# Attention tiles and upper banks in two pools each, and heads kind by kind

## The chip, the cores and the metric

One core of a Trainium2 chip runs the kernel. The metric is the device time of one execution in microseconds (us). The core has a matrix engine (TensorE, "PE" in the profile, with its weight loads as "PEld"), three engines for elementwise work (VectorE "DVE", ScalarE "ACT", GpSimd "POOL"), and a queue that issues transfers (SyncE, "SP"). Tiles live in SBUF; matmuls write PSUM, which has eight banks of 2 KB per partition.

## What is computed

Two layers of a streaming encoder over 1024 tokens of width 1024. Each layer runs three groups of four attention heads on one input projection, then attention over 256 memory tokens, then an MLP:

```python
for layer in range(DEPTH):
    h = rms_norm(x, mix_norm_g[layer])
    proj = h @ w_in[layer]
    da_q, da_k, da_v, sb_q, sb_k, sb_v, c_q, c_kv, k_r = jnp.split(proj, pts, axis=-1)
    y_a = diff_attention(da_q, da_k, da_v, rel_bias, da_q_norm_g[layer], da_k_norm_g[layer],
                         da_lambda[layer], da_subln_g[layer], layer)
    y_b = stick_breaking(sb_q, sb_k, sb_v, sb_out_g[layer])
    y_c = latent_attention(c_q, c_kv, k_r, pos, mla_cq_norm_g[layer], mla_ckv_norm_g[layer],
                           w_mla_uq[layer], w_mla_ukv[layer], mla_q_norm_g[layer],
                           mla_k_norm_g[layer], mla_out_g[layer])
    y = jnp.concatenate([y_a, y_b, y_c], axis=-1)
    x = x + y @ w_out[layer]
    h = rms_norm(x, memx_norm_g[layer])
    x = x + memory_attention(h, mem, mem_norm_g[layer], w_mem_q[layer], w_mem_kv[layer],
                             mem_q_norm_g[layer], mem_k_norm_g[layer], w_mem_o[layer])
    h = rms_norm(x, ffn_norm_g[layer])
    x = x + jnp.square(jax.nn.relu(h @ w_ff1[layer])) @ w_ff2[layer]
```

Differential attention takes softmax(map 0) - lam * softmax(map 1) and latent attention one softmax, each over the keys of earlier and the own chunk of 64. Stick-breaking attention uses a sigmoid and a running product instead of a softmax:

```python
log_beta = jax.nn.log_sigmoid(z)
log_1m_beta = jnp.where(earlier, jax.nn.log_sigmoid(-z), 0.0)
later = lax.cumsum(log_1m_beta, axis=3, reverse=True) - log_1m_beta
a = jnp.where(earlier, jnp.exp(log_beta + later), 0.0)
```

## The kernel before

**Two halves.** The 1024 tokens are eight tiles of 128 rows; half h = 0 is tiles 0 to 3, half 1 tiles 4 to 7. Half 0 attends to 512 keys at most, half 1 to 1024. A layer runs, in the order in which it is written: `project(0)`, the norm of half 1, the memory's keys and values (`memory`), `project(1)`, `attention(0)`, `merge(0)` (output projection and memory attention of half 0), `attention(1)`, `merge(1)`, and the MLP. The projections write queries, keys and values to DRAM (`dqk`, `sqk`, `mqk`, `dv`, `sv`, `mv`), and each head loads its own from there. Weights come as raw fp32 tiles of 128x512 (`raw`) and are split on ScalarE and VectorE into a high and a low part (lines 562 and 563), so that three matmuls make one product (`mm3`, lines 584 to 586).

**The order of each engine is made when the program is built.** `order_engines` (line 227) takes all instructions with their dependences and gives each engine a fixed list, by a list scheduling with estimated costs (`_cost`, line 192). Among the instructions that are ready it takes the one of lowest rank (`mem.rank`), and of equal rank the one that was written first. A layer's projection of half 0 has rank 0, merge(0) 9, attention(0) 10, project(1) 20, attention(1) 40, merge(1) 50 and the MLP 60. So project(1) fills the gaps of attention(0), and the first ten groups of the MLP on half 0 fill those of attention(1): `ff1` and `ff2` with the banks s2 and s3. The engines work through their lists in order.

**Places in SBUF.** Pools are stacked from two sides: left ones upward, right ones downward. A pool that is opened on the place of a closed one may be written only when the old one's uses are over; `order_engines` lets the first write of each tile wait for all uses of the closed pools under its pool (lines 112 and 281), and the chip's own waits go tile by tile. Above the fixed pools the kernel has 85.5 KB per partition. The inputs of the projections and of the MLP are one 32 KB tile for each half: `h0` at the left end, `h1` at the right end. The merge has a pool `mw` of 21 KB left, above h0.

- `attention(0)` has one pool, at0, of 39 KB on the left: over h0's place and 7 KB beyond.
- `attention(1)` has one pool, at1, of 52 KB on the right: over h1's place and over most of mw's.

In such a pool the tiles are: kst (keys of a head, 4 buffers in half 0, 6 in half 1), v (values, 2 or 3), o (queries, high and low part, and the bias of a differential head, 6 or 7), and in half 0 also p (3) and at (2) for the weights and their transposes; in half 1 these two come from the ring t4 of the fixed pools. A differential head takes 2 kst, 5 o and 1 v, a stick-breaking head 1, 2 and 1, a latent head 2, 2 and 1. Buffers are taken in turn.

**Banks.** Four banks (s0 to s3) are fixed. The upper four are one pool, `more` (lines 385 to 387): e0 to e3 during attention(0) and both projections, d0 and d1 of two banks each during attention(1) and the MLP. attention(0) and merge(0) use e0 and e1, the projection of half 1 and the memory e2 and e3.

**A head.** For each tile of its half: scores on TensorE (line 1019) into e0 or e1 (half 1: d0 or d1). Differential: a bias on the last 256 keys (1098, its tile loaded at 1086), the maximum (1099), Exp on ScalarE (1101), both maps joined (1107). Stick-breaking: two Sigmoids on ScalarE (1124, 1125), a scan on VectorE (1129), products on GpSimd (1128, 1131). Latent: maximum (1150), Exp (1153). Then transposes (605), a copy or a split by ScalarE and VectorE (1037, 597, 598), weighting (1039, 1054 to 1057) and a norm (1073 to 1076). The loads are at lines 980 (kst), 986 (latent kst and o), 992 (o) and 999 (v). Lines 1161 to 1163 run the twelve heads in turn by kind: head d of each kind, then head d + 1.

Of the kernel before, what the change touches and what calls it, by code (L numbers as in the profile page):

```python
# [9 lines left out]
F32 = mybir.dt.float32  # L10
F32R = mybir.dt.float32r
# [3 lines left out]
PSUM = bass.MemoryType.PSUM  # L15
DRAM = bass.MemoryType.DRAM

P = 128
# [331 lines left out]
def trunk(ctx: ExitStack, mem: Mem, tc: tile.TileContext, a: dict, out: bass.AP):  # L350
    nc = tc.nc
    HT = NT // 2
    HS = S // 2
# [8 lines left out]
    def f(ap):  # L362
        return ap.bitcast(F32)
# [13 lines left out]
    psp = Pool("psum", space=PSUM)  # L377
# [2 lines left out]
    turn = {}  # L380
    ALL, FRONT, BACK = ("s0", "s1"), ("s0", "s1", "d0", "d1"), ("s2", "s3")
    EARLY, SIDE = ("s0", "s1", "e0", "e1"), ("e2", "e3")
    more = [None, None]

    def open_banks():
        more[0] = ExitStack()
        more[1] = Pool("more", space=PSUM, st=more[0])

    def close_banks():
        more[0].close()  # L390
# [1 line left out]
    def bank(cls):  # L392
        k = turn.get(cls, 0)
        turn[cls] = k + 1
        tag = cls[k % len(cls)]
        if tag[0] == "d":
            return more[1].tile([P, 1024], F32, tag=tag)[:, :512]
        return (psp if tag[0] == "s" else more[1]).tile([P, 512], F32, tag=tag)

    def banks2(cls=("d0", "d1")):  # L400
        k = turn.get(cls, 0)
        turn[cls] = k + 1
        return more[1].tile([P, 1024], F32, tag=cls[k % len(cls)])

    open_banks()

# [223 lines left out]
    def close_h(h):  # L630
        hst[h].close()
# [26 lines left out]
    for l in range(L):  # L658
# [286 lines left out]
        t2ring[0] = (0, 1)  # L945
        km, vm = memory(SIDE, hm)
        project(1, BACK, SIDE)
        close_h(0)
        close_h(1)


        y = {}

        def attention(h, ap_):
            NK = HT * (h + 1)
            KS = HS * (h + 1)
            for t in tiles(h):
# [4 lines left out]
            def ptile():  # L962
                if h:
                    return f(tp.tile([P, 1024], F32R, tag="t4", ring=(0, 1, 2)))
                return ap_.tile([P, KS], F32, tag="p", bufs=3)

            def attile():
                if h:
                    return tp.tile([P, 1024], F32R, tag="t4", ring=(3, 4)).rearrange("p (s c) -> p s c", s=2)
                return ap_.tile([P, 2, 512], F32R, tag="at", bufs=2)  # L970

            def small():
                return cp.tile([P, 8], F32, tag="sm", bufs=8)

            def stack(src, r0, r1, rows):

                k = ap_.tile([P, KS], F32R, tag="kst", bufs=bufs["kst"])
                for u in range(h + 1):
                    for o, r in ((0, r0), (rows, r1)):
                        dma(f(k[o:o + rows, u * HS:(u + 1) * HS]), src[u][r:r + rows])  # L980
                return k

            def block(src, r0, rows, tag, bufs, width=None):
                k = ap_.tile([P, width or KS], F32R, tag=tag, bufs=bufs)
                for u, s in enumerate(src):
                    dma(f(k[:rows, u * HS:(u + 1) * HS]), s[r0:r0 + rows])
                return k

            def twice(src, r0, rows):
                k = ap_.tile([P, HS], F32R, tag="o", bufs=bufs["o"])  # L990
                for o in (0, rows):
                    dma(f(k[o:o + rows]), src[r0:r0 + rows])
                return k

            def values(src, c0, dt):

                v = ap_.tile([P, NK, P], F32R, tag="v", bufs=bufs["v"])
                for u in range(h + 1):
                    dma(f(v[:, u * HT:(u + 1) * HT, :]),
                        src[u].rearrange("(t p) c -> p t c", p=P)[:, :, c0:c0 + P])  # L1000
                return v if dt == F32R else f(v)
# [41 lines left out]
            def weighted64(t, pa, v, yo, scale):  # L1043

                po = bank(("s1",))
                pv = po[:, :256].rearrange("p (s c) -> p s c", s=2)
                for b0, nb, pt in turned(t, pa):
                    w = nb * P
                    at = attile()
                    split(pt[:, :w], at[:, 0, :w], at[:, 1, :w])  # L1050
                    for j in range(b0, b0 + nb):
                        c = slice((j - b0) * P, (j - b0 + 1) * P)
                        if h:
                            nc.tensor.matmul(pv, v[:, j, :], at[:, :, c], start=j == 0, stop=j == t)  # L1054
                        else:
                            nc.tensor.matmul(po[:, :P], at[:, 0, c], v[:, j, :], start=j == 0, stop=False)
                            nc.tensor.matmul(po[:, :64], at[:, 1, c], v[:, j, :64], start=False, stop=j == t)
                if h:

                    u = ap_.tile([P, P], F32, tag="u", bufs=2)  # L1060
                    nc.scalar.activation(u, po[:, :P], AF.Copy)
                    nc.vector.tensor_tensor(u[:64], po[:64, P:256], u[:64], op=ALU.add)
                    nc.tensor.matmul(po[:, 256:320], u, twin, start=True, stop=True)
                    nc.scalar.activation(yo, po[:, 256:320], AF.Copy, scale=scale)
                else:
                    nc.scalar.activation(yo, po[:, 64:128], AF.Copy, scale=scale)
                    nc.vector.scalar_tensor_tensor(yo, po[:, :64], scale, yo, op0=ALU.mult, op1=ALU.add)

            def norm_y(t, c, e, sm, gain):

                yo = y[t][:, c:c + e]
                jk = ap_.tile([P, P], F32, tag="jk", bufs=2)
                nc.scalar.activation(jk[:, :e], yo, AF.Square, accum_out=sm)
                nc.vector.tensor_scalar(sm, sm, 1.0 / e, EPS, op0=ALU.mult, op1=ALU.add)  # L1074
                nc.gpsimd.tensor_tensor(sm, sm, mhalf[:, :1], op=ALU.pow)  # L1075
                nc.vector.scalar_tensor_tensor(yo, yo, sm, gain, op0=ALU.mult, op1=ALU.mult)

            def da_head(d):
                ks, qh, ql = [], [], []
                for m in range(2):  # L1080
                    r0 = d * P + m * 64
                    ks.append(stack([dqk[u][1] for u in range(h + 1)], r0, 4 * P + r0, 64))
                    qh.append(twice(dqk[h][0], r0, 64))
                    ql.append(twice(dqk[h][0], 4 * P + r0, 64))
                b = f(ap_.tile([P, HS], F32R, tag="o", bufs=bufs["o"])).rearrange("p (m k) -> p m k", m=2)
                dma(b, biasd[2 * d:2 * d + 2].rearrange("m p k -> p m k"))
                vt = values(dv, d * P, F32)
                for t in tiles(h):
                    n = (t + 1) * P
                    cq = slice((t % HT) * P, (t % HT + 1) * P)  # L1090
                    sm = small()
                    pm = []
                    for m in range(2):
                        ps = scores(t, [(qh[m][:, cq], ks[m]), (ql[m][:, cq], ks[m])])

                        w = min(n, 256)
                        near = ps[:, n - w:n]
                        nc.vector.tensor_tensor(near, near, b[:, m, 256 - w:], op=ALU.add)
                        nc.vector.tensor_reduce(sm[:, m:m + 1], ps[:, :n], axis=AX.X, op=ALU.max, negate=True)  # L1099
                        pt = ptile()  # L1100
                        nc.scalar.activation(pt[:, :n], ps[:, :n], AF.Exp, bias=sm[:, m:m + 1],
                                             accum_out=sm[:, 2 + m:3 + m])
                        pm.append(pt)
                    nc.vector.reciprocal(sm[:, 4:6], sm[:, 2:4])
                    nc.vector.scalar_tensor_tensor(sm[:, 6:7], sm[:, 2:3], sm[:, 5:6], neglam[:, l:l + 1],
                                                   op0=ALU.mult, op1=ALU.mult)
                    nc.vector.scalar_tensor_tensor(pm[0][:, :n], pm[1][:, :n], sm[:, 6:7], pm[0][:, :n],
                                                   op0=ALU.mult, op1=ALU.add)
                    po = weighted(t, pm[0], vt)
                    nc.scalar.activation(y[t][:, d * P:(d + 1) * P], po, AF.Copy, scale=sm[:, 4:5])  # L1110
                    norm_y(t, d * P, P, sm[:, 7:8], rows3[0])
# [45 lines left out]
                    weighted64(t, pt, vs, y[t][:, c:c + 64], sm[:, 3:4])  # L1157
                    norm_y(t, c, 64, sm[:, 7:8], rows3[2])


            for d in range(4):
                for head in (sb_head, da_head, mla_head) if h else (sb_head, mla_head, da_head):
                    head(d)

        def merge(h, cls, km, vm, gx, gf, omp):
# [161 lines left out]

        with ExitStack() as st:
            mem.rank(R + 10)
            attention(0, Pool("at0", st=st))  # L1330
        open_h(0)
        mem.rank(R + 9)
        gx = growload(a["memx_norm_g"][l])
# [10 lines left out]
        open_banks()  # L1344
        with ExitStack() as st:
            mem.rank(R + 40, late=300.0)
            attention(1, Pool("at1", st=st, side="right"))
        open_h(1)
        with ExitStack() as st:
            mem.rank(R + 50)  # L1350
# [124 lines left out]
```

## Time and profile before

| | us |
|---|---|
| median of 3 runs | 2913.85 |
| lowest, highest | 2912.05, 2920.17 |
| the profiled execution | 2916.28 |
| its span, first to last instruction | 2914.2 |

The profile is of one execution. Busy time counts an engine's instructions; PEclk is the TensorE clock that was granted, as a share of full speed. Where time goes by stage (length of the stage, then busy us):

| stage of layer 0 | from, to us | TensorE | VectorE | ScalarE |
|---|---|---|---|---|
| project(0), memory | 0 to 163 | 148.14 | 112.39 | 91.22 |
| attention(0), rest of project(1), merge(0) | 365 to 497 | 131.13 | 89.78 | 73.16 |
| merge(1) and MLP | 835 to 1000 | 162.76 | 106.40 | 76.56 |
| MLP, and project(0) of layer 1 | 1000 to 1603 | 603.00 | 343.93 | 203.38 |

A row of a wait names the engine and line that waited, what released it, the time in all, how often, and the longest. In a timeline, a bracket at the end of a row tells how long the engine had stood idle before it and what ended that.

### The profile page before, as it was taken

How to read it: one execution, taken by the hardware profiler on the slowest of the kernel's cores; microseconds unless marked ns; L12 is line 12 of the kernel's file. 1: busy time of each engine (PE TensorE's matmuls, PEld its weight loads, DVE VectorE, ACT ScalarE, POOL GpSimd, SP SyncE). 2: the span in 40 equal slices, each digit the busy share in tenths (PEclk: the TensorE clock that was granted, in tenths of full speed). 3: DMA queues.
4: the chain of work that ended last, by engine and by line, in shares of the span. 5: the costliest groups of instructions: out<-in, count | busy, mean ns of one | idle time of the engine just before them, and what ended most of it. 6: DMA issues, size and time to landing. Idle time of an engine off the chain costs nothing.

```text
span 2914.2 us, 41564 instructions
## 1 busy us (share of the span) xinstructions
PE 2820.8 (97%) x14642; PEld 2382.1 (82%) x14642; DVE 1941.8 (67%) x3708; ACT 1434.6 (49%) x3262; POOL 447.0 (15%) x524
## 2 busy tenths in 40 slices
PE   7999999899999999999999999998999999999999
PEld 6878788778888888888898778887888888888887
DVE  5868776788867644565568787767888575444555
ACT  5667655566645312233345775656666453222332
POOL 1423321122201000000013332211222010000000
PEclk9999999999999999999999999999999999999999
DMA  7776544634232211223356664365441412112232
GB/s 232 213 202 185 170 131 132 181 108 128 84 125 66 80 40 48 72 75 107 95 174 204 199 201 148 111 177 140 130 125 61 138 37 73 58 44 73 87 102 90
DMA packets 362912, 352.91 MB, mean 121 GB/s; under 512 B 26616, under 2 KB 264480, under 8 KB 362704
## 3 DMA queue, kind: packets, MB, share of 16 engines
q1 hardware_dynamic: 362704, 350.25, 40.0%
q8 instruction: 116, 1.90, 0.3%
q14 instruction: 92, 0.75, 0.1%
HBM read 290.33 MB, written 59.83 MB: 120 GB/s over the span
## 4 chain that ended last, share of the span: by engine, by line
PE 77%; DVE 8%; ACT 7%; DMA 4%; issue 2%; POOL 2%; SPq 1%; DVEq 0%; ACTq 0%; POOLq 0%
PE d L1305 16%; PE s L586 12%; PE s L585 12%; PE s L584 11%; PE s L1305 5%; PE s L605 4%; PE d L1019 3%; PE e L586 2%; PE e L584 2%; PE e L585 2%; PE s L1039 1%; PE e L605 1%; DVE sm L1099 1%; PE s L1054 1%; PE e L1019 1%
## 5 line engine op out<-in xcount | busy, mean ns | idle before, releaser
L562 ACT ACTIVATE w<-raw 128x512 fp32r<-128x512 f32 (+1 forms) x704 | 430.5, 626 | 607.1 <-PE d L1305 232.7
L563 DVE TENSOR_TENSOR w<-raw,w 128x512 fp32r<-128x512 f32 (+1 forms) x704 | 475.8, 690 | 233.6 <-ACT w L562 232.2
L584 PE MATMUL s<-h,w 128*128 128x512 f32 x1120 | 443.3, 396 | 0.4 <-DVE x L1309 0.4
L586 PE MATMUL s<-h,w 128*128 128x512 f32 x1120 | 442.8, 395 | 0.0
L585 PE MATMUL s<-h,w 128*128 128x512 f32 x1120 | 442.5, 395 | 0.0
L1309 DVE TENSOR_TENSOR x<-d,x 128x1024 f32<-128x1024 f32 x177 | 215.3, 1217 | 159.0 <-PE d L1305 159.0
L1305 PE MATMUL s<-w,hid 128*128 128x512 f32 x960 | 271.8, 407 | 11.8 <-DVE x L1309 5.9
L592 POOL TENSOR_TENSOR ms<-ms,mhalf 128x8 f32<-128x8 f32 (+3 forms) x112 | 128.2, 1149 | 987.8 <-DVE ms L590 984.9
L584 PE MATMUL s<-w,h 128*128 128x512 f32 (+2 forms) x672 | 248.2, 372 | 1.8 <-ACT w L562 1.7
L585 PE MATMUL s<-w,h 128*128 128x512 f32 (+2 forms) x672 | 247.0, 369 | 0.8 <-DVE w L563 0.7
L586 PE MATMUL s<-w,h 128*128 128x512 f32 (+2 forms) x672 | 245.8, 367 | 0.0
L1282 ACT ACTIVATE r<-s 128x512 f32<-128x512 f32 x128 | 76.4, 597 | 343.7 <-issue 206.2
L1305 PE MATMUL d<-w,hid 128*128 128x512 f32 x1056 | 244.8, 389 | 0.0
L1305 PE MATMUL d<-w,t 128*128 128x512 f32 x1056 | 244.2, 389 | 0.0
L586 PEld LDWEIGHTS s<-h,w 128*128 128x128 f32 x1120 | 211.3, 189 | 40.1
L584 PEld LDWEIGHTS s<-h,w 128*128 128x128 f32 x1120 | 211.1, 188 | 40.2 <-DVE x L1309 1.1
L585 PEld LDWEIGHTS s<-h,w 128*128 128x128 f32 x1120 | 211.3, 189 | 39.1
L1284 DVE TENSOR_TENSOR r<-r 128x512 f32<-128x512 f32 x128 | 92.4, 722 | 224.7 <-ACT r L1282 224.4
L1305 PEld LDWEIGHTS d<-w,t 128*128 128x128 f32 x1056 | 198.2, 188 | 41.1
L1305 PEld LDWEIGHTS d<-w,hid 128*128 128x128 f32 x1056 | 198.1, 188 | 41.1
L1075 POOL TENSOR_TENSOR sm<-sm,mhalf 128x1 f32<-128x1 f32 x192 | 123.4, 643 | 596.8 <-DVE sm L1074 521.8
L1305 PEld LDWEIGHTS s<-w,hid 128*128 128x128 f32 x960 | 168.9, 189 | 47.1 <-DVE x L1309 11.2
(332 smaller groups left out, 5440.1 us busy)
## 6 DMA issues: line engine op xcount, KB each, us to landing
raw<-in_w_ff SPq DMA_DIRECT2D x416, 256.0 KB
raw<-in_w_in SPq DMA_DIRECT2D x144, 256.0 KB
raw<-in_w_out SPq DMA_DIRECT2D x64, 256.0 KB
x<-in_x SPq DMA_DIRECT2D x16, 512.0 KB
raw<-in_w_in SPq DMA_DIRECT2D x32, 208.0 KB
v<-sv SPq DMA_DIRECT2D x24, 256.0 KB
v<-mv SPq DMA_DIRECT2D x24, 256.0 KB
v<-dv SPq DMA_DIRECT2D x24, 256.0 KB
```

What stands on the lines that cost most here:

```text
L562: nc.scalar.activation(w[:, 0, o], raw, AF.Copy)
L563: nc.vector.tensor_tensor(w[:, 1, o], raw, f(w[:, 0, o]), op=ALU.subtract)
L584: nc.tensor.matmul(ps, sh, mh, start=start, stop=False)
L585: nc.tensor.matmul(ps, sh, ml, start=False, stop=False)
L586: nc.tensor.matmul(ps, sl, mh, start=False, stop=stop)
L592: nc.gpsimd.tensor_tensor(rs, ms, mhalf[:, :n], op=ALU.pow)
L605: nc.tensor.transpose(ps[:, k * P:(k + 1) * P], src[:, k * P:(k + 1) * P], ident)
L1019: nc.tensor.matmul(ps[:, c:c + w], sta, mov, start=first, stop=last[c // 512] == i)
L1075: nc.gpsimd.tensor_tensor(sm, sm, mhalf[:, :1], op=ALU.pow)
L1284: nc.vector.tensor_tensor(r2, r, r, op=ALU.mult)
L1305: nc.tensor.matmul(parts[e], hd[i][:, s, tt], w[:, e * 512:(e + 1) * 512], start=first, stop=last)
L1309: nc.vector.tensor_tensor(xt[t][:, cols], ps, xt[t][:, cols], op=ALU.add)
```

## The change

Four things are done.

- The upper banks become two pools: one holds e0, e1 and d0, the other e2, e3 and d1.
- `attention` gets two pools, `first` and `rest`. A buffer of a ring with a number below `FIRST` lies in `first`: all 4 kst, both v and 4 of 6 o in half 0; 2 of 6 kst, 1 of 3 v and 4 of 7 o in half 1. Everything else lies in `rest`. The rings are as long as before.
- For half 0, `first` (20 KB) is opened on the right below h1, in the space between h0 and h1, before h0 is closed; `rest` (19 KB) lies over h0's place. h1 is closed after attention(0). For half 1, `first` (20 KB) lies on the left above h0, where mw was, and `rest` (32 KB) over h1's place.
- The four heads of a kind run one after the other: in half 0 stick-breaking, latent, differential; in half 1 stick-breaking, differential, latent.

```diff
--- before.py
+++ after.py
@@ -380,11 +380,15 @@
     turn = {}
     ALL, FRONT, BACK = ("s0", "s1"), ("s0", "s1", "d0", "d1"), ("s2", "s3")
     EARLY, SIDE = ("s0", "s1", "e0", "e1"), ("e2", "e3")
-    more = [None, None]
+    more = [None, {}]
 
     def open_banks():
+
         more[0] = ExitStack()
-        more[1] = Pool("more", space=PSUM, st=more[0])
+        more[1] = {}
+        for tags in (("e0", "e1", "d0"), ("e2", "e3", "d1")):
+            p = Pool("more", space=PSUM, st=more[0])
+            more[1].update((t, p) for t in tags)
 
     def close_banks():
         more[0].close()
@@ -394,13 +398,14 @@
         turn[cls] = k + 1
         tag = cls[k % len(cls)]
         if tag[0] == "d":
-            return more[1].tile([P, 1024], F32, tag=tag)[:, :512]
-        return (psp if tag[0] == "s" else more[1]).tile([P, 512], F32, tag=tag)
+            return more[1][tag].tile([P, 1024], F32, tag=tag)[:, :512]
+        return (psp if tag[0] == "s" else more[1][tag]).tile([P, 512], F32, tag=tag)
 
     def banks2(cls=("d0", "d1")):
         k = turn.get(cls, 0)
         turn[cls] = k + 1
-        return more[1].tile([P, 1024], F32, tag=cls[k % len(cls)])
+        tag = cls[k % len(cls)]
+        return more[1][tag].tile([P, 1024], F32, tag=tag)
 
     open_banks()
 
@@ -945,13 +950,21 @@
         t2ring[0] = (0, 1)
         km, vm = memory(SIDE, hm)
         project(1, BACK, SIDE)
-        close_h(0)
-        close_h(1)
 
 
         y = {}
 
-        def attention(h, ap_):
+        def attention(h, first, rest):
+
+            FIRST = {"kst": 2 if h else 4, "v": 1 if h else 2, "o": 4}
+            turns = {}
+
+            def at_(shape, dt, tag, bufs):
+                k = turns.get(tag, 0)
+                turns[tag] = k + 1
+                k %= bufs
+                return (first if k < FIRST.get(tag, 0) else rest).tile(shape, dt, tag=tag, ring=(k,))
+
             NK = HT * (h + 1)
             KS = HS * (h + 1)
             for t in tiles(h):
@@ -962,39 +975,39 @@
             def ptile():
                 if h:
                     return f(tp.tile([P, 1024], F32R, tag="t4", ring=(0, 1, 2)))
-                return ap_.tile([P, KS], F32, tag="p", bufs=3)
+                return at_([P, KS], F32, tag="p", bufs=3)
 
...
@@ -1157,9 +1170,8 @@
                     weighted64(t, pt, vs, y[t][:, c:c + 64], sm[:, 3:4])
                     norm_y(t, c, 64, sm[:, 7:8], rows3[2])
 
-
-            for d in range(4):
-                for head in (sb_head, da_head, mla_head) if h else (sb_head, mla_head, da_head):
+            for head in ((sb_head, da_head, mla_head) if h else (sb_head, mla_head, da_head)):
+                for d in range(4):
                     head(d)
 
         def merge(h, cls, km, vm, gx, gf, omp):
@@ -1327,7 +1339,10 @@
 
         with ExitStack() as st:
             mem.rank(R + 10)
-            attention(0, Pool("at0", st=st))
+            first = Pool("at0a", st=st, side="right")
+            close_h(0)
+            attention(0, first, Pool("at0b", st=st))
+        close_h(1)
         open_h(0)
         mem.rank(R + 9)
         gx = growload(a["memx_norm_g"][l])
@@ -1344,7 +1359,8 @@
         open_banks()
         with ExitStack() as st:
             mem.rank(R + 40, late=300.0)
-            attention(1, Pool("at1", st=st, side="right"))
+            first = Pool("at1a", st=st)
+            attention(1, first, Pool("at1b", st=st, side="right"))
         open_h(1)
         with ExitStack() as st:
             mem.rank(R + 50)
```

More of the change, by code (lines that the diff above doesn't have):

```diff
@@ L969, in attile @@
                     return tp.tile([P, 1024], F32R, tag="t4", ring=(3, 4)).rearrange("p (s c) -> p s c", s=2)
-                return ap_.tile([P, 2, 512], F32R, tag="at", bufs=2)
+                return at_([P, 2, 512], F32R, tag="at", bufs=2)
             def small():
@@ L975, in stack @@
             def stack(src, r0, r1, rows):
-                k = ap_.tile([P, KS], F32R, tag="kst", bufs=bufs["kst"])
+                k = at_([P, KS], F32R, tag="kst", bufs=bufs["kst"])
                 for u in range(h + 1):
@@ L983, in block @@
             def block(src, r0, rows, tag, bufs, width=None):
-                k = ap_.tile([P, width or KS], F32R, tag=tag, bufs=bufs)
+                k = at_([P, width or KS], F32R, tag=tag, bufs=bufs)
                 for u, s in enumerate(src):
@@ L989, in twice @@
             def twice(src, r0, rows):
-                k = ap_.tile([P, HS], F32R, tag="o", bufs=bufs["o"])
+                k = at_([P, HS], F32R, tag="o", bufs=bufs["o"])
                 for o in (0, rows):
@@ L995, in values @@
             def values(src, c0, dt):
-                v = ap_.tile([P, NK, P], F32R, tag="v", bufs=bufs["v"])
+                v = at_([P, NK, P], F32R, tag="v", bufs=bufs["v"])
                 for u in range(h + 1):
@@ L1058, in weighted64 @@
                 if h:
-                    u = ap_.tile([P, P], F32, tag="u", bufs=2)
+                    u = at_([P, P], F32, tag="u", bufs=2)
                     nc.scalar.activation(u, po[:, :P], AF.Copy)
@@ L1071, in norm_y @@
                 yo = y[t][:, c:c + e]
-                jk = ap_.tile([P, P], F32, tag="jk", bufs=2)
+                jk = at_([P, P], F32, tag="jk", bufs=2)
                 nc.scalar.activation(jk[:, :e], yo, AF.Square, accum_out=sm)
@@ L1084, in da_head @@
                     ql.append(twice(dqk[h][0], 4 * P + r0, 64))
-                b = f(ap_.tile([P, HS], F32R, tag="o", bufs=bufs["o"])).rearrange("p (m k) -> p m k", m=2)
+                b = f(at_([P, HS], F32R, tag="o", bufs=bufs["o"])).rearrange("p (m k) -> p m k", m=2)
                 dma(b, biasd[2 * d:2 * d + 2].rearrange("m p k -> p m k"))
```

## The prediction

> **What bounds the kernel now.** I read the page first, then the busy time by stage, then who waited for whom in each stage, and last the timelines of ScalarE and of the DMA queue at the two places where TensorE stops longest.
>
> ```profile
> span 2914.2 us, 41564 instructions
> PE 2820.8 (97%) x14642; PEld 2382.1 (82%) x14642; DVE 1941.8 (67%) x3708; ACT 1434.6 (49%) x3262; POOL 447.0 (15%) x524
> ```
>
> TensorE works 97% of the span, and the change removes no matmul: 2914.2 - 2820.8 = 93.4 us of idle TensorE, plus what its lowered clock costs, is all that can be won. Where it lies, by stage:
>
> ```profile
> core 0: us, PE busy (x) PEld busy (x) DVE busy (x) ACT busy (x) POOL busy (x), PEclk, DMA share, GB/s
> 163.00:365.00 202.00, 185.72 (x1071) 158.63 (x1070) 158.77 (x478) 146.19 (x441) 73.87 (x103) 0.97 0.60 179
> 497.00:540.00 43.00, 33.26 (x162) 27.41 (x161) 26.48 (x44) 21.82 (x40) 11.70 (x10) 0.90 0.77 213
> 540.00:835.00 295.00, 285.03 (x1636) 242.79 (x1634) 241.08 (x486) 189.97 (x456) 63.04 (x69) 1.00 0.38 111
> 1603.00:1800.00 197.00, 181.81 (x1071) 155.81 (x1070) 156.33 (x474) 147.93 (x444) 71.83 (x100) 0.98 0.63 189
> 1940.00:1980.00 40.00, 31.23 (x155) 25.37 (x154) 24.73 (x41) 21.21 (x39) 11.71 (x10) 0.94 0.81 221
> 1980.00:2280.00 300.00, 291.65 (x1665) 248.46 (x1664) 244.93 (x493) 193.59 (x465) 63.59 (x70) 0.99 0.38 113
> ```
>
> Columns: length, busy time of each engine, granted clock, DMA share. Each layer has three stages with idle TensorE. **A**, attention of the first half beside the projection of the second: 202 - 185.72 = 16.3 us in layer 0, 15.2 in layer 1. **B**, the first 40 us of attention of the second half: 9.7 and 8.8. **C**, the rest of it: 10.0 and 8.3. Together 31.5 + 18.5 + 18.3 = 68.3 us, and everything that the change touches lies there. The clock below 1 costs busy time times what is missing: A 185.72 x 0.03 + 181.81 x 0.02 = 9.2, B 33.26 x 0.10 + 31.23 x 0.06 = 5.2, C 291.65 x 0.01 = 2.9 us.
>
> What TensorE waited for, in A and then in B (the latter with a little of C):
>
> ```profile
> PE e L1019 <- ACT p L1101: 3.7, 4, 1.2
> PE e L1019 <- ACT p L1153: 3.7, 6, 1.1
> ...
> PE e L1019 <- DMA o<-sqk00q: 0.7, 2, 0.4
> ```
>
> ```profile
> PE d L1019 <- ACT t L1101: 7.6, 1, 7.6
> ...
> PE d L1019 <- DMA o<-sqk01q: 1.4, 1, 1.4
> ```
>
> In A the score matmuls (L1019) wait for the exponentials that free their bank, 7.4 us in layer 0, never over 1.2 us at once. Layer 1 has the first of these rows word for word, and for the second
>
> ```profile
> PE e L1019 <- ACT p L1153: 3.5, 6, 1.1
> ```
>
> which makes 7.2. What stands in front of these exponentials is in ScalarE's groups and timeline:
>
> ```profile
> L1124 ACT ACT_TABLE_LOAD x22 | 28.2, 1283 | 2.7 <-DVE p L1107 2.4
> L1101 ACT ACT_TABLE_LOAD x14 | 18.0, 1283 | 0.3
> L1153 ACT ACT_TABLE_LOAD x8 | 10.3, 1283 | 0.9 <-DVE sm L1151 0.9
> ```
>
> ```profile
> 205.63 1.28 ACT L1124 ACT_TABLE_LOAD   x1
> 206.92 0.28 ACT L1124 ACTIVATE p<-e 128x128 f32<-128x128 f32 x1
> 207.09 0.48 ACT L1037 ACTIVATE at<-s 128x384 f32<-128x384 f32 x1
> 207.60 1.28 ACT L1101 ACT_TABLE_LOAD   x1
> 208.89 0.69 ACT L1101 ACTIVATE p<-e,sm 128x512 f32<-128x512 f32 x1
> ...
> 211.56 1.28 ACT L1124 ACT_TABLE_LOAD   x1
> ```
>
> A stick-breaking head uses Sigmoid (L1124), the other two kinds Exp (L1101, L1153), and each crossing costs a load of 1283 ns: 44 in all, 22 a layer. With the kinds in turn every round crosses, and where a differential head ends and the next stick-breaking head begins, the two are interleaved and cross three times within 6 us, as shown. The order of each engine is fixed when the program is built, by costs (line 202) that charge nothing for a load, so every load makes ScalarE late against the order that the others follow.
>
> In B one wait holds most. ScalarE stood still there, and the DMA queue says why:
>
> ```profile
> 531.01 0.63 ACT L562 ACTIVATE w<-raw 128x512 fp32r<-128x512 f32 x1 [7.19 <-DMA raw<-in_w_ff]
> ```
>
> ```profile
> 496.50 1.09 SPq L980 DMA_DIRECT2D kst<-sqk00k  x2
> ...
> 527.03 11.61 SPq L559 DMA_DIRECT2D raw<-in_w_ff  x5
> ```
>
> From 496.5 to 527 the queue issues nothing but loads of heads. The MLP weights that the filler work needs come behind them, ScalarE waits 7.19 us for the first, and the exponential that frees the score bank is queued behind that conversion.
>
> **The change part by part.**
>
> *Order of heads (1161-1163).* All four stick-breaking heads come first, then the two Exp kinds. Sigmoid is entered once and left once in each of the four attentions: 8 loads instead of 44, 36 x 1.283 = 46 us less on ScalarE. At single crossings the trace has one load each, so I take 2 for an attention; 4 would leave 28 x 1.283 = 36 us. Most of it lies beside other work: TensorE stood idle for the exponentials in A for 7.4 + 7.2 = 14.6 us. Of these I take two thirds, **10 us**, because some of the exponentials would also be late without a load; the bounds are 0 (another wait ends as late) and 14.6. In C, from 640 us on, such waits are small,
>
> ```profile
> PE d L1019 <- ACT t L1101: 1.1, 2, 0.8
> ```
>
> and I take **3 us** for both layers; bounds 0 and 18.3.
>
> The Trainium skill, "ScalarE: Activation LUTs", section "What ACT_TABLE_LOAD costs", gives each switch a drain of about 1380 ns besides the load. In the rows above the load starts 0.03 us after the work before it and the next activation 0.01 us after the load, so the trace shows no drain, and I do not count it; by the page ScalarE would save about 96 us instead of 46, and the estimate for A would stand at its upper bound.
>
> *Clock in A and B.* After short idle times the clock falls to half:
>
> ```profile
> 178.00:180.00 2.00, 0.86 (x5) 0.51 (x5) 0.73 (x4) 1.97 (x6) 1.25 (x2) 1.00 0.79 237
> 188.00:190.00 2.00, 2.00 (x12) 1.99 (x12) 1.69 (x7) 1.44 (x6) 0.70 (x2) 0.50 0.71 220
> ```
>
> An idle microsecond at 178, at a table load (A's first Exp), is followed 8 us later by half clock. With fewer gaps I take back 5 of A's 9.2 us and 4 of B's 5.2: **9 us**; bounds 0 and 14.4. The Trainium skill, "TensorE: Matmul & The Clock Gate", section "HAM oscillation — how this bites in real kernels", names idle gaps above about 3.4 us as what throttles again. By it A's dips would not hang on such short gaps and would stay, and the sum would be 5 us smaller; here the gap before the dip is 1.14 us, so the trace speaks against it.
>
> *Attention tiles in two pools.* For the second half, the first two key tiles (kst), the first value tile and four of the query tiles (o) now lie where the merge of the first half had its weights, instead of all lying over that place and over the projection's input together. The last read of the merge's weights is at 470.6, and now the loads began at 496.5, when the projection ended:
>
> ```profile
> 470.64 0.39 PE L586 MATMUL s<-w,t 128*128 128x512 f32 x1
> ```
>
> ```profile
> kst<-dqk00k SPq DMA_DIRECT2D x32, 128.0 KB
> o<-biasd SPq DMA_DIRECT2D x16, 256.0 KB
> v<-sv SPq DMA_DIRECT2D x24, 256.0 KB
> ```
>
> A kst tile of this half is 4 transfers of 128 KB, an o tile 2 of 128, a v tile 2 of 256. Before, the burst held a stick-breaking head (1536 KB), a differential one (2816), a latent one (1664, its keys in 192 KB pieces) and two key tiles (1024): 7040 KB. After, a full set of rings is 6 x 512 + 7 x 256 + 3 x 512 = 6400 KB, of which 2 x 512 + 4 x 256 + 512 = 2560 KB may go 26 us earlier, beside the projection's end. 3840 KB are left; at B's 213 GB/s that is 18 us instead of 33, so the MLP weights come some 12 us earlier, which is more than the stall of 7.6. I take three quarters of B's idle time, **14 of 18.5 us**. Bounds: 18.5 as the gain, and 0, if the loads that go earlier delay the weights there and the stall comes earlier and as long; longer it should not be, with fewer bytes in all.
>
> For the first half, keys, values and four of six o tiles lie free of the projection's input (tiles p and at do not), so loads of the first two heads are there when it ends. A's wait for sqk00q, 0.7 us and as much in layer 1, goes: **1.5 us**; what ScalarE and VectorE gain by an earlier start is in A's other terms.
>
> *Upper PSUM banks in two pools.* d0 now waits for e0 and e1 alone, d1 for e2 and e3. That lets the first score matmul of the second half run before the projection's last transposes; TensorE has projection matmuls then, so it is worth nothing by itself, at most the 1.4 us that L1019 waits for sqk01q, which are in B. At the end of a layer it frees two banks a tile earlier, where TensorE does not idle: 0. Closing order and the names cost no instruction.
>
> *What is late next.* Differential heads now follow each other. Each takes 5 o tiles of a ring of 7 (6 in the first half), so part of the next head's queries and its bias (L1086) wait for the last scores of the head before; its first bias addition then waits for a transfer. Such a transfer with its wait lasts, by the chain that ended last:
>
> ```profile
> 182.20 4.26 DMA o<-biasd
> ```
>
> There are 3 such borders in each of 4 attentions, 12. What waited for such loads before:
>
> ```profile
> DVE e L1098: 0.7, 1
> ```
>
> Hidden behind the end of the old head a border costs 0; not hidden at all 4.26, together 51 us. I take 0.7 us each, **-8 us**, near the hidden end, because the old head's last maximum, exponential, transposes and weighting follow its last scores, and because all 16 bias loads made VectorE wait 0.7 us once before.
>
> **The sum.** 10 + 3 + 9 + 14 + 1.5 - 8 = 29.5 us. The profiled execution took 2916.28 us (its span 2914.2 and 2.1 around it), which gives 2886.8; the median of the runs shown is 2913.85, 2.4 lower, which gives 2884.4. I say **2886**.
>
> **The rivals.**
>
> *More comes back.* If the late exponentials were the root of nearly all idle time, A, B and C give two thirds of 68.3 and of the clock's 17.3, 57 us: 2859. For it: most waits in A are on ScalarE. Against: C has 9 us of idle time a layer spread over many short waits that no load precedes.
>
> *It does not do what it says, or ScalarE was not the bound.* The queue still sends all loads of heads ahead of the weights, only earlier, and the stall moves ahead of 497; VectorE, at 158.77 of 202 us in A, holds the exponentials' inputs as long as the loads did. Then only some 5 to 8 us remain: 2908 to 2911. For it: VectorE is busier than ScalarE in every stage. Against: the named waits are on ScalarE.
>
> *Slower: the borders between differential heads.* The SP queue is in order, so a bias load that waits for the last scores holds all weights behind it, and VectorE, in order too, holds the filler's conversions behind the bias addition. Unhidden this is 12 x 4.26 = 51 us against gains of 37.5: 2930. It turns to a loss at 37.5 / 12 = 3.1 us a border. For it: rings of 7 and 6 against 5 tiles a head. Against: the keys, values and first queries are there ahead, and a head's end lasts several us.
>
> **How the numbers follow.** About 0.3% (8.7 us) is what a measurement of this kernel can tell from no change: faster means under 2905, slower over 2922.6. Forecast, 2872 to 2900: 0.47. More comes back, around 2859: 0.13. Little remains, 2900 to 2922: 0.23, of which 0.08 below 2905. Slower: 0.17. So faster 0.68, same 0.15, slower 0.17. Leaving out the far ends of the first and last rival, the range is 2856 to 2924; the forecast's own is 2872 to 2900.
>
> **What would show it.** Right: 8 to 16 table loads, and no run of three; loads of keys issued before the end of the projection (about 475 to 496), no ScalarE wait of several us for in_w_ff near 530, granted clock 1.00 in B; A's idle TensorE near 10 us a layer. Wrong: waits of L1098 for o<-biasd of 2 us or more at the start of differential heads, with weights queued behind; idle TensorE before 497 that was not there; A's idle time unchanged with the loads gone, then VectorE set it.

## The result and the profile after

The changed kernel takes 2875.89 us (median of 4 runs, 2872.78 to 2878.94); the kernel before, on the same chips, 2916.17 us. The ratio is 0.9858, with a 95% interval of 0.9847 to 0.9870: 40 us less. The profiled execution's span is 2871.9 us, 42.3 us shorter than before.

The page after, its span and its row of busy times:

```profile
span 2871.9 us, 41672 instructions
PE 2809.7 (98%) x14642; PEld 2377.7 (83%) x14642; DVE 1955.5 (68%) x3708; ACT 1387.7 (48%) x3226; POOL 449.6 (16%) x524
```

TensorE has the same 14642 matmuls; its idle time fell from 93.4 to 62.2 us and its busy time by 11.1 us, which make the 42.3. ScalarE has 36 instructions less and 46.9 us less to do: 36 x 1.283 = 46.2. They are the crossing loads, eight of which are left. (In the code after, most lines are some 13 higher: scores at 1032, Sigmoids at 1137 and 1138, the Exps at 1114 and 1166, head loads at 993, 1005 and 1012, raw weights at 564.)

```profile
L1137 ACT ACT_TABLE_LOAD x4 | 5.1, 1283 | 0.1
L1166 ACT ACT_TABLE_LOAD x2 | 2.6, 1283 | 0.0
L1114 ACT ACT_TABLE_LOAD x2 | 2.6, 1283 | 0.0
```

The stages A, B and C after, cut where the attention of each half begins, as before (length, busy time of PE, PEld, DVE, ACT, POOL, clock, DMA share, GB/s):

```profile
163.00:355.00 192.00, 180.90 (x1074) 155.52 (x1073) 163.10 (x480) 132.04 (x432) 72.94 (x103) 0.97 0.59 182
480.00:525.00 45.00, 40.45 (x198) 32.67 (x196) 34.61 (x50) 26.05 (x54) 16.91 (x15) 0.92 0.66 197
525.00:820.00 295.00, 290.12 (x1668) 248.57 (x1669) 248.26 (x499) 187.67 (x459) 60.68 (x66) 1.00 0.39 118
1587.00:1790.00 203.00, 192.47 (x1127) 165.37 (x1126) 168.54 (x489) 135.22 (x437) 73.00 (x103) 0.98 0.58 178
1905.00:1945.00 40.00, 35.84 (x174) 28.89 (x173) 30.34 (x45) 24.06 (x47) 15.59 (x14) 0.91 0.65 197
1945.00:2245.00 300.00, 295.42 (x1697) 253.22 (x1696) 251.57 (x503) 189.66 (x463) 62.09 (x67) 1.00 0.40 119
```

Idle TensorE in A is 11.1 and 10.5 us (16.3 and 15.2 before), in B 4.6 and 4.2 (9.7 and 8.8), in C 4.9 and 4.6 (10.0 and 8.3). Each stage gave 9 to 10 us over both layers. The clock in A and B hardly changed.

The DMA queue shows the early loads, in A and in B:

```profile
100.64 1.12 SPq L993 DMA_DIRECT2D kst<-sqk00k  x2
```

```profile
456.79 1.09 SPq L993 DMA_DIRECT2D kst<-sqk00k  x2
...
505.95 1.23 SPq L993 DMA_DIRECT2D kst<-dqk01k  x2
507.28 14.73 SPq L564 DMA_DIRECT2D raw<-in_w_ff  x7
```

The first half's loads begin at 100.6 instead of 162, the second's at 456.8 instead of 496.5. The MLP weights that had to wait until 527 are issued at 507; ScalarE still waits for them, 5.0 us at once instead of 7.2:

```profile
510.63 0.63 ACT L567 ACTIVATE w<-raw 128x512 fp32r<-128x512 f32 x1 [4.99 <-DMA raw<-in_w_ff]
```

### The profile page after: what moved, and what is told of

It is laid out like the page before. It is cut to its first block, busy times and chain, and to the rows that moved or that the text cites. A ratio compares the mean times of both kernels' runs of the same rounds, so it can differ in the third digit from the quotient of the medians.

```text
span 2871.9 us, 41672 instructions
## 1 busy us (share of the span) xinstructions
PE 2809.7 (98%) x14642; PEld 2377.7 (83%) x14642; DVE 1955.5 (68%) x3708; ACT 1387.7 (48%) x3226; POOL 449.6 (16%) x524
## 4 chain that ended last, share of the span: by engine, by line
PE 85%; DVE 5%; DMA 3%; ACT 3%; issue 2%; POOL 1%; SPq 1%; DVEq 0%; ACTq 0%; POOLq 0%
PE d L1317 17%; PE s L589 13%; PE s L590 13%; PE s L591 13%; PE s L1317 6%; PE s L610 4%; PE d L1032 3%; PE e L589 2%; PE e L591 2%; PE e L590 2%; PE s L1052 2%; PE s L1067 2%; DMA raw<-in_w_in 2%; PE e L610 1%; PE e L1032 1%
## 5 line engine op out<-in xcount | busy, mean ns | idle before, releaser
L1296 DVE TENSOR_TENSOR r<-r 128x512 f32<-128x512 f32 x128 | 98.4, 769 | 219.0 <-ACT r L1294 218.3
```

What stands on the lines that cost most here:

```text
L1296: nc.vector.tensor_tensor(r2, r, r, op=ALU.mult)
```

## The experiments

Twelve kernels ran, each against the kernel before on the same chip. The change has three parts (order of heads, SBUF pools, PSUM banks), and a table load can be taken away without touching the order: with Sigmoid in place of Exp in the heads that use Exp, all heads share one table. What these heads give is then another function, so such a kernel serves only to read the time.

| kernel | order | SBUF pools | banks | loads | us | ratio, 95% interval |
|---|---|---|---|---|---|---|
| before | in turn | one | one | 44 | 2917 to 2918 | 1 |
| e1_order | by kind | one | one | 8 | 2912.5 | 0.9983, 0.9973 to 0.9994 |
| e2_pools | in turn | two | one | 44 | 2908.4 | 0.9980, 0.9967 to 0.9993 |
| e3_banks | in turn | one | two | 44 | 2916.0 | 0.9997, 0.9987 to 1.0008 |
| e4_one_table | in turn | one | one | 8 | 2891.5 | 0.9918, 0.9899 to 0.9937 |
| e5_no_banks | by kind | two | one | 8 | 2877.3 | 0.9860, 0.9842 to 0.9877 |
| e9_order_banks | by kind | one | two | 8 | 2912.6 | 0.9979, 0.9967 to 0.9991 |
| e10_pools_banks | in turn | two | two | 44 | 2907.0 | 0.9964, 0.9949 to 0.9978 |
| e6_after_one_table | by kind | two | two | 8 | 2880.5 | 0.9875, 0.9856 to 0.9894 |
| e11_half1_pools | by kind | two in half 1 | two | 8 | 2890.3 | 0.9903, 0.9889 to 0.9918 |
| e12_half0_pools | by kind | two in half 0 | two | 8 | 2900.6 | 0.9938, 0.9920 to 0.9956 |
| e13_turn_one_table | in turn | two | two | 8 | 2870.9 | 0.9838, 0.9823 to 0.9853 |
| e8_short_ring | by kind | two | two | 8 | 2868.2 | 0.9832, 0.9816 to 0.9847 |

(The eight loads of the one-table kernels lie where the attention's Sigmoid and the memory attention's Exp meet.)

**Each part alone.**

```diff
-            for d in range(4):
-                for head in (sb_head, da_head, mla_head) if h else (sb_head, mla_head, da_head):
+            for head in ((sb_head, da_head, mla_head) if h else (sb_head, mla_head, da_head)):
+                for d in range(4):
                     head(d)
```

> The kernel before with the new order of heads alone. Theory (order and pools each bring their own part: the order fewer table loads and with them stages A and C, the pools stage B): 8 crossing loads, idle TensorE in A near 11 us a layer and in C near 5, B near 9 us a layer as before because all loads of heads still start when the projection has ended; 2892 to 2900 us. Rival (the pools brought all of it, the loads were hidden): 8 loads but within 6 us of before, 2910 to 2920.

Measured: 8 loads, and yet only 5 us (0.9983). This is the rival's number, but not its reason: the loads were not hidden. As the next kernels show, the order lost elsewhere what it gained. In A the blocks of head loads follow each other and the weights for the filler wait behind them. The DMA queue, ScalarE and TensorE of this kernel, around 180 us:

```profile
161.45 1.39 SPq L980 DMA_DIRECT2D kst<-sqk00k  x2
...
178.54 0.58 SPq L986 DMA_DIRECT2D kst<-mqk00k  x1
...
179.59 1.31 SPq L559 DMA_DIRECT2D raw<-in_w_in  x3
```

```profile
182.80 0.55 ACT L562 ACTIVATE w<-raw 128x416 fp32r<-128x416 f32 x1 [2.09 <-DMA raw<-in_w_in]
```

```profile
183.40 0.77 PE L584 MATMUL s<-w,h 128*128 128x416 f32 x2 [1.74 <-ACT w L562]
```

```profile
180.00:190.00 10.00, 6.83 (x29) 5.58 (x29) 6.91 (x18) 6.25 (x21) 5.70 (x9) 0.69 0.52 163
```

From 161 to 179 the queue sends all four stick-breaking heads; TensorE then does its filler late, idles 3.2 of 10 us, and the clock falls to 0.69. In the changed kernel the same four heads' keys are there before, and this window reads

```profile
180.00:190.00 10.00, 9.61 (x61) 8.44 (x59) 9.76 (x29) 8.48 (x30) 7.43 (x11) 1.00 0.38 112
```

The SBUF pools alone keep the loop in turn:

> The kernel before with the two SBUF pools of each attention and the moved closings alone; heads in turn, upper banks in one pool. Theory: 44 crossing loads, A and C as before, B near 4 us a layer instead of 9; 2900 to 2908 us. Rival (order and pools only work together: with heads in turn the first loads that go early are those of one head of each kind, and the burst stays): 2912 to 2918.

Measured: 0.9980, some 6 us. The median, 2908.4, is at the slow edge of what was expected, but the runs spread from 2904 to 2920, and by the ratio the gain lies between the theory's numbers and the rival's. The first scores of the second half come at 496.1 (504.1 before), and B idles 7.7 and 7.0 us, not 4; A and C keep their loads.

The banks alone have only the edits of `open_banks`, `bank` and `banks2`:

> The kernel before with the upper banks in two pools alone. Theory: no engine waits for these banks, so no change: 2911 to 2920 us. Rival (scores of the second half start earlier and fill idle time in B): B under 6 us a layer, 2905 or less.

Measured: 0.9997, no change. So the parts alone give 5, 6 and 1 us, 12 in all, of 40.

**What a table load costs.** The kernel before, with one word changed at each Exp of the heads:

```diff
-nc.scalar.activation(pt[:, :n], ps[:, :n], AF.Exp, bias=sm[:, m:m + 1],
+nc.scalar.activation(pt[:, :n], ps[:, :n], AF.Sigmoid, bias=sm[:, m:m + 1],
```

> The kernel before, heads in turn, with Sigmoid in place of Exp in the differential and latent heads, so that what these heads give is another function; every instruction keeps its size and place, only the crossing loads go (two a layer stay for each entry of the memory attention). Theory (table loads are what the order takes away): A near 11 us idle a layer, C near 5, B as before; 2890 to 2900 us, as near to the order alone as 5 us. Rival (the order of heads helps by what it does to loads of keys and to the lists, not by the tables): within 6 us of before.

Measured: 0.9918, 24 us, in the middle of the theory's numbers; that it would lie within 5 us of the order alone was wrong by 16. A and B of layer 0 and A of layer 1:

```profile
169.00:350.00 181.00, 171.25 (x1039) 148.92 (x1039) 154.89 (x473) 126.17 (x423) 72.33 (x103) 0.99 0.63 191
492.00:532.00 40.00, 32.74 (x165) 27.32 (x166) 27.18 (x47) 19.71 (x43) 12.27 (x11) 0.91 0.68 188
1600.00:1783.00 183.00, 172.64 (x1031) 150.04 (x1031) 155.41 (x473) 125.87 (x422) 72.90 (x103) 0.97 0.62 187
```

A idles 9.8 and 10.4 us instead of 16.3 and 15.2, and B keeps 7.3 of its 9.7 us. So 36 loads cost 24 us, 0.66 us each, and the order by kind, which removes the same 36, costs 19 us by itself in the old pools (0.9983 against 0.9918).

Where these 19 us lie shows between e4 and e1, which have the same number of loads. TensorE's idle time grows from 79.2 to 87.7 us and its busy time from 2810.8 to 2821.9. Weighted over stretches of 5 us, the busy time lost to a lowered clock grows from 14.6 to 29.7 us, and most of that is in A (6.5 and 19.0). So the order's price is for the larger part the clock. A of e1 in both layers:

```profile
168.00:360.00 192.00, 178.71 (x1043) 156.52 (x1042) 158.41 (x474) 129.38 (x425) 73.54 (x103) 0.94 0.60 180
1603.00:1800.00 197.00, 180.01 (x1051) 157.23 (x1050) 159.31 (x475) 131.62 (x427) 73.60 (x103) 0.94 0.60 182
```

In each layer the clock falls twice: behind the block of stick-breaking loads, as shown above, and once more among the differential heads (in layer 0, 0.66 from 305 to 310).

**What the parts do together.** Next came two parts at a time, and the changed kernel with one table.

> The changed kernel with the upper banks in one pool again; order and SBUF pools as changed. Order alone gave 5 us and pools alone 6, the whole change 40. Theory (the banks carry what is missing: with one pool the first scores of the second half wait for the projection's last use of e2 and e3, and the early loads cannot be used): first score matmul of the second half near 496 us as with the pools alone instead of 484.6, B's idle time near 7 us; 2893 to 2908 us. Rival (order and SBUF pools together make it, the banks are nothing): first score near 485, 2872 to 2880 us.

> The kernel before with the new order and the upper banks in two pools; SBUF pools as before. Theory (each of banks and SBUF pools holds back the other, so two of three give little): loads of heads begin only at the projection's end, near 496; within 4 us of the order alone, 2906 to 2916. Rival (the SBUF pools are nothing once order and banks are there): 2872 to 2885.

Measured: 0.9860 and 0.9979. Order and SBUF pools make the whole gain, the banks none: my theory that the banks carried what was missing fell, and in e5 the first score of the second half is at 485.3 with the banks in one pool.

> The changed kernel with the heads in turn again. 44 crossing loads are back, which cost 24 us with the old pools (the kernel before without the loads ran at 0.9918). Theory (order = loads, and the early start is worth about 15 us by itself): 2896 to 2904 us, first scores of the second half near 485. Rival (the early start needs the order by kind, because the first loads of a round in turn are more than the early tiles hold): 2906 to 2914.

> The changed kernel with Sigmoid in place of Exp in the differential and latent heads, so that what these heads give is another function; the last crossing load inside each attention goes, one or two a layer stay at the memory attention. Theory (what the loads still cost after the change is 4 x 1.3 us, half of it covered): 2868 to 2876 us, within 4 us of the changed kernel. Rival (the change of kind itself, with its waits, is what is left in A): A idle time unchanged near 11 us a layer.

e10 is the changed kernel with the loop above taken back. Measured: 2907.0 (runs from 2893 to 2913), the rival's number, with the first scores of the second half at 497 and not at 485: SBUF pools and banks do little for the time while the heads come in turn with their loads. The rival's reason is not shown by that, for the loads go early here too, and the weights follow at 517 instead of 527:

```profile
469.65 1.09 SPq L993 DMA_DIRECT2D kst<-sqk00k  x2
...
517.30 10.80 SPq L564 DMA_DIRECT2D raw<-in_w_ff  x5
```

What is long is A, before these scores: TensorE idles 18.4 and 17.9 us there, and 9.9 and 9.3 in e13 below, which is e10 without the loads. The changed kernel with one table came out at 2880.5 against an expected 2868 to 2876. It spares the four loads inside the attentions, but has four at the memory attention in their place, and that exchange gains nothing; A idles 10.5 and 9.8 us, as the rival had it.

**Whether the order is good by itself.** The loop in turn, new pools, one table:

> The changed kernel with the heads in turn again and Sigmoid in place of Exp in the differential and latent heads, so that what these heads give is another function: pools as changed, order as before, crossing loads gone. In turn with the loads it was 2907.0. Theory (the loads cost 24 us with the new pools as with the old): 2880 to 2888 us, so that the order by kind is worth the loads and little more. Rival (the order by kind is better by itself once loads of heads go early): 2895 or more. Other rival (the order is worse by itself and hidden by the pools): 2872 or less.

Measured: 2870.9 us (0.9838), below the lowest number of the theory and within the other rival's: the order is worse by itself. It is 36 us less than in turn with the loads (2907.0), 1.0 us for each of 36 loads, and its first scores of the second half come at 481.1, so in turn they can be early too. The changed kernel is 5 us above it, but the two intervals overlap. The clean comparison is e6, which differs in the order alone: 9.6 us above, with intervals that just do not meet. So the order by kind is good for the loads alone; its own price, 19 us in the old pools, is about 10 us in the new ones. It is again the clock: TensorE idles less in e6 than in e13 (63.2 and 68.3 us) but loses 17 instead of 7 us to a lowered clock.

**Which half's pools.** The changed kernel, with one attention put back into one pool, here the first half's:

```diff
-            first = Pool("at0a", st=st, side="right")
             close_h(0)
-            attention(0, first, Pool("at0b", st=st))
-        close_h(1)
+            close_h(1)
+            first = Pool("at0", st=st)
+            attention(0, first, first)
```

> The changed kernel with attention of the first half in one pool as before; order, upper banks and the second half's two pools as changed. With the order and no SBUF pools the kernel is at 2912.6, with all at 2875.9. Theory (each half's pools mend its own stage: the first half's A, the second half's B and C): A loses 20 us of both layers again (idle 13 to 17 and clock 7 to 11 a layer), B and C as in the changed kernel; 2890 to 2898 us. Rival (one half's pools make it all, the rest of the time moves with the start): under 2882, or over 2906.

and the second half's:

```diff
-            first = Pool("at1a", st=st)
-            attention(1, first, Pool("at1b", st=st, side="right"))
+            first = Pool("at1", st=st, side="right")
+            attention(1, first, first)
```

> The changed kernel with attention of the second half in one pool as before; order, upper banks and the first half's two pools as changed. Theory: A as in the changed kernel (idle near 11 and clock 3 to 4 a layer), B near 8 and C near 8 as with the order alone; 2890 to 2898 us. Rival: under 2882, or over 2906.

Measured: 2890.3 and 2900.6, against 2912.6 with neither and 2875.9 with both: the second half's pools give 22 us, the first half's 12, which adds up to the 37 of both nearly. e12 came out 2.6 us above its numbers. A of e11 in layers 0 and 1:

```profile
168.00:362.00 194.00, 179.54 (x1045) 156.76 (x1045) 158.50 (x474) 129.75 (x425) 73.95 (x103) 0.94 0.59 177
1601.00:1793.00 192.00, 176.66 (x1045) 154.91 (x1046) 158.36 (x474) 129.81 (x425) 73.48 (x103) 0.96 0.60 181
```

and B and C of layer 0 in e12:

```profile
494.00:534.00 40.00, 30.79 (x150) 25.51 (x151) 24.71 (x40) 18.33 (x38) 15.69 (x13) 0.87 0.70 202
534.00:807.00 273.00, 264.16 (x1518) 227.13 (x1517) 230.45 (x456) 172.09 (x418) 58.27 (x63) 0.99 0.38 112
```

Each half's pools mend their own stages: without the first half's, A idles 14.5 and 15.3 us at a clock of 0.94 and 0.96; without the second's, B idles 9.2 and C 8.8 us.

**The block of loads in B.** The ring of keys of the second half shortened:

```diff
-bufs = {"kst": 6, "v": 3, "o": 7} if h else {"kst": 4, "v": 2, "o": 6}
+bufs = {"kst": 4, "v": 3, "o": 7} if h else {"kst": 4, "v": 2, "o": 6}
```

> The changed kernel with 4 instead of 6 key tiles in the second half's ring, so that the block of head loads ahead of the MLP weights is 1 MB shorter. Theory (the idle time left in B, 4.5 and 4.3 us, is the wait for those weights behind the block): the first weights some 5 us earlier, B near 1 to 2 us a layer, C unchanged; 2868 to 2874 us. Rival (differential heads need the longer ring: keys of the next head come late): waits of L1032 for kst in C, 2878 or more.

Measured: 2868.2 us (0.9832), the theory's number and the lowest median of all. The weights are issued 6 us earlier, and B in both layers reads

```profile
501.32 15.43 SPq L564 DMA_DIRECT2D raw<-in_w_ff  x6
```

```profile
484.00:524.00 40.00, 37.85 (x201) 30.44 (x199) 34.80 (x53) 25.99 (x54) 20.71 (x17) 1.00 0.71 195
1904.00:1944.00 40.00, 37.46 (x201) 30.72 (x200) 33.99 (x52) 26.32 (x55) 20.73 (x17) 1.00 0.70 192
```

2.2 and 2.5 us idle instead of 4.6 and 4.2, and full clock. A shorter prefetch is 7.7 us faster here by the medians, though its interval and the changed kernel's touch at 0.9847.

## Why the prediction was right, and where its terms were not

The forecast was 29.5 us less, the measured gain is 40, inside the range. Point by point:

- **The loads.** 8 of 44 are left, as counted, and A's idle time fell by 9.9 us (10 and 1.5 forecast). The drain of some 1380 ns at each switch that the Trainium skill gives ("ScalarE: Activation LUTs", section "What ACT_TABLE_LOAD costs") shows nowhere: ScalarE stood idle for 3.9 us in all before the 44 loads (the three rows of loads in the prediction), and its busy time fell by the 46.9 us of the loads and not by 96. But I treated the order as if it only removed loads. Removing them is worth 24 us (e4) to 36 us (e13); ordering by kind costs 19 us in the old pools, and that price the sum did not have. It stayed small only because of the pools. The sum also added the parts as if each stood alone; alone they give 5, 6 and 1 us, together 40.
- **B.** 14 us forecast, 9.8 measured. The stall became shorter (5.0 us instead of 7.2) and did not go. The weights came 20 us earlier, more than the 12 I had worked out, but so did the stage: I had held its start fixed. First and last score matmul of the second halves, before and after:

```profile
L1019 PE MATMUL d<-kst,o x576: 274/389/796, 504.1 to 2254.7; 128*128 128x512 f32 x66, 128*128 128x384 f32 x36, 96*128 96x512 f32 x28, 128*128 128x256 f32 x26
```

```profile
L1032 PE MATMUL d<-kst,o x576: 274/389/775, 484.6 to 2201.4; 128*128 128x512 f32 x62, 128*128 128x384 f32 x36, 96*128 96x512 f32 x32, 128*128 128x256 f32 x30
```

  The first is at 484.6 instead of 504.1, 19.5 us earlier, so that the filler runs out of weights earlier too. The mechanism was right: e8 shortens the block and the idle time follows.
- **C and the borders between differential heads.** 3 us of gain in C and 8 us of loss at the borders (half of them in A) forecast, 8.8 us of gain in C measured: the largest miss. The bias loads are later than before, as the slower rival said, but never long. What ended VectorE's waits at the bias addition (line 1111 after):

```profile
DVE e L1111 <- DMA o<-biasd: 3.5, 4, 1.2
...
DVE d L1111 <- DMA o<-biasd: 0.2, 1, 0.2
```

  3.7 us in all, in 16 heads, at most 1.2 at once where I had bounded a border by 4.26; no wait of TensorE for a bias is among the largest. The other half of that rival, weights held behind a head's loads, shows once in A of layer 0. The queue, ScalarE, TensorE and the stretch after:

```profile
276.85 0.34 SPq L564 DMA_DIRECT2D raw<-in_w_in  x1
...
287.32 0.53 SPq L1099 DMA_DIRECT2D o<-biasd  x1
...
291.57 0.70 SPq L564 DMA_DIRECT2D raw<-in_w_in  x1
```

```profile
298.05 0.63 ACT L567 ACTIVATE w<-raw 128x512 fp32r<-128x512 f32 x1 [1.04 <-DMA raw<-in_w_in]
```

```profile
299.44 2.07 PE L1032 MATMUL e<-kst,o 128*128 128x384 f32 x4 [2.16 <-ACT p L1114]
```

```profile
300.00:305.00 5.00, 4.26 (x13) 2.53 (x12) 4.54 (x12) 3.14 (x11) 2.15 (x4) 0.50 0.35 104
```

  From 281.5 to 290.3 the queue issues nothing but loads of a differential head. ScalarE then waits for weights, TensorE 2.16 us for the Exp behind them, and the clock falls to 0.50. This one dip makes nearly all of the 4.1 us of clock that A of layer 0 still loses; the sum had priced the borders by waits alone.

  I had argued that C's idle time is many short waits that no load precedes. C's gain hangs on the loads all the same (e4, without any change of order, has 5.9 and 7.4 us of idle time there) and on the second half's pools (8.8 us left in e12). How pools opened at B still help 100 us later was not traced.
- **The clock.** 9 us forecast, in A and B. Weighted over stretches of 5 us, the busy time lost to a lowered clock is 17.7 us before and 14.4 after: 3 us. In A it fell by 2.4 us and in B it rose by 2.8, so the two stages of the forecast gave nothing together; the 3 us are C's, which lost 3.6 to the clock before and nothing after, and for which none was forecast. The clock of 1.00 that I had named for B did not come (0.92 and 0.91). A gap of 3.61 us there (7.55 before) was still followed by 0.52:

```profile
511.42 1.22 PE L1067 MATMUL s<-t,v 128*128 128x256 f32 x4 [3.61 <-ACT x L1077]
```

```profile
510.00:515.00 5.00, 3.58 (x12) 2.83 (x13) 3.22 (x8) 3.79 (x10) 1.40 (x2) 0.52 0.52 152
```

  In e10, by contrast, the 40 us from 497 idle 7.8 us in gaps of at most 2.46 us, at a clock of 1.00. The rule of gaps above about 3.4 us (the Trainium skill, "TensorE: Matmul & The Clock Gate", section "HAM oscillation — how this bites in real kernels") would have kept A's part of this term at nothing, about as far from the measured 2.4 us as my 5. B's two gaps agree with the rule; the half clock in A after a gap of 1.14 us, shown in the prediction, speaks against its figure.
- **The banks.** 0 forecast and measured (e3, and e5 against the change).
- **What the sum did not have.** TensorE's busy time fell by 8 us beyond the clock. No one part carries it: without the clock's loss the busy time is 2803 us before and with the banks alone, 2797 with the pools alone, 2796 without the loads, 2792 with the order alone and 2795 after. Its cause stays open.

So the result lies in the range, and the mechanisms of the loads and of the weights behind the head loads were right, but the sum came near by luck, by errors against each other: it left out the price of the order and took too much for the clock and B, and it took too little for C and nothing for the busy time.

## What to carry to other kernels

Before grouping work by kind to save table loads, take the loads away without touching the order (one function for all) and so price both apart: here the order cost most of what the loads gave until the data of its first heads could come early. Where one queue carries urgent loads and the filler's weights, look at how large a block the ring lets the urgent ones make; a shorter ring can be the faster one. An order with no more idle time can still be slower by the clock that its gaps cost, so count the lowered clock beside the idle time. Parts of a change that give little alone can give most together, so a part's worth is to be measured with the others in place and not only by itself.

## What had not been expected

The same 36 loads cost 0.66 us each with the old pools and 1.0 us with the new, near their full 1.283 us, though ScalarE is busy under half of the span; why they cost more there was not traced. And an identical count of matmuls has 11.1 us less busy time after the change, of which the granted clock explains 3.
